# A hybrid encoder layer: where the first norm's scale is applied, and who orders TensorE in the first stage

## The chip, the cores and the metric

The kernel runs on one core of a Trainium2 chip. The metric is device time in microseconds (us) of one execution, with all inputs in device memory at the start. A core has TensorE (PE in the profile; its weight loads are PEld), VectorE (DVE), ScalarE (ACT), GpSimd (POOL) and SyncE (SP, which here only issues transfers). Each engine works through its own list of instructions in order; between engines, semaphores say when an operand is ready.

## The reference, cut to what matters

The layer is applied to 2048 prompt positions and, with the same weights, to 256 sample positions; the width is 1024.

```python
h = rmsnorm(x, norm1_w)                    # x * rsqrt(mean(x*x) + eps) * norm1_w
p = h @ w_in                               # mq, mk, mv, mo, gates, aq, ak, av
m_out = mlstm_mixer(mq, mk, mv, mo, gates, b_gates, mh_norm_w)   # 8 heads, both directions
a_out = attention_mixer(aq, ak, av, q_norm_w, k_norm_w)          # 8 heads, 2 kv heads, rotary
x = x + concat([m_out, a_out]) @ w_out
h = rmsnorm(x, norm2_w)
u = centred_dwconv(h @ w_up, conv_w, conv_b)
a, g = split(u, 2)
y = rmsnorm(x + (silu(g) * a) @ w_down, final_norm_w)
```

One head of the mLSTM, in one direction, at position l: with weights Dw and iw from the gates, and a state (C, n) carried over chunks,

```python
s = (q @ k.T) * Dw
num = iw * (q @ C) + s @ v
den = iw * (q @ n) + s.sum(-1)
h = num / max(abs(den), exp(-m))
out = sigmoid(mo) * rmsnorm_per_head(h_forward + h_backward) * mh_norm_w
```

The norm's scale r = rsqrt(mean(x*x) + eps) is one number for each position, and norm1_w one for each input column. So `(x*r*w1) @ W` is `r * (x @ (w1*W))`: r may be applied to x ahead of the products, or to the products' rows behind them.

## The kernel before, in words

All products are in float32 split into two parts: a high part (`fp32r`) and the remainder, and a product is the sum of three matmuls (high by high, high by low, low by high). The 2304 positions are 18 tiles of 128. The two sample tiles (16 and 17) come first, then the prompt tiles 0 to 15; x lies in memory transposed, so that a tile is [128 columns, 8 chunks, 128 positions].

**The first stage** (`phase_a`) works tile by tile. `front_a` loads x, squares it on ACT (L186), sums the eight chunks on POOL (`xq`, `sq`, L192, L193; for the first tile on DVE, L189), sums over partitions by a matmul with ones (`rs_a`, L131), takes the power -0.5 on POOL (`rcol_a`, L135) and spreads the result over all partitions by a second matmul with the identity (L142). `front_b` multiplies x by it on DVE (L200), makes the high part on ACT (L201) and the low part on DVE (L202), both called `n1T`, and stores them to memory for the mLSTM. `mm` projects a tile onto 800 columns (the attention's q, k, v and the gates, weights `w_a`) as 24 matmuls of 512 columns and 24 of 288 into `pj`, which has two buffers. `post_a` takes `pj` out of PSUM (`qk`, `v`, the gate columns `gtm`) and has the mean squares of the heads (`ms`, L267) turned into `rqk` on POOL (L100, L101). `post_b` scales by it (`xh`, L273), applies the rotary tables (`t`, L282 to L288) and splits the result (`qz`, L290, L291). `post2` turns the keys by PE (`pk`, L326); `gates` takes logarithms and turns the gates into rows (`pg`, L319). Into the same stage fall the split of the mLSTM's first weights (`wm`, L108 and L112) and the scaling of the rotary tables (`tab`, L232, mostly on POOL).

**The second stage** interleaves attention (`px`: score maxima, reduced by L570; `ps`: scores, L595 and L596; `pv`: values, L613) with the mLSTM in four passes of two heads. A pass projects all tiles again from the stored `n1T` (`proj`: `mj` holds k and q, `mv` holds v and the output gate), updates states (`upd`, `recur`), and produces outputs in steps `out_a` to `out_d`: products `mS`, `mI`, `mN` in one small PSUM pool (`pm`, tag "m", two buffers), a division and a norm on DVE, ACT and POOL (L886 to L919), and a turn `mT` with the gate applied (`mmx`, L931). The last pass (`p == LASTP`) projects transposed (`proj_kv`, `proj_qo`), so that its gate `ogT` has positions along the free axis. **Then** attention alone goes on beside the output projection (`po`), and the feed-forward stages (`pa` to `pd`) follow.

The order of the instructions on each engine is set when the program is built: a scheduler goes through the written program with modelled times and priorities and picks, on each engine, what is ready first. Where a scope says `manual_schedule` for PE, PE keeps the order of the source; before the change that scope begins only with the part in which attention runs alone.

## Time and profile before

| | |
|---|---|
| median of 3 runs | 3428.69 us (3424.76 to 3433.05) |
| the profiled execution's own time | 3428.88 us |
| its span, first to last instruction | 3427.2 us |
| PE busy | 3329.3 us (97%) |
| DVE busy | 2677.3 us (78%) |
| ACT busy | 1931.2 us (56%) |
| POOL busy | 1120.9 us (33%) |
| mean granted TensorE clock | 0.990 |

A busy time is the union of an engine's instructions; consecutive ones overlap a little, so the distance from start to start is the better measure of what one costs in a row of many. In lists of instructions, `[0.69 <-DVE mx L570]` says that the engine stood idle for 0.69 us before this one and that DVE's `mx` ended the wait. A row of a window table gives its length, then busy time and number of instructions of each engine, the granted clock, and the share and rate of the transfers.

### The profile page before, as it was taken

The page shows a single profiled execution, that of the slowest core. Times are in us where ns is not written, and L with a number is a line of the kernel's source. Part 1 is how long each engine was busy: PE and PEld are TensorE (multiplying, and loading weights), DVE is VectorE, ACT ScalarE, POOL GpSimd, SP SyncE. Part 2 cuts the span into 40 slices and gives each one's busy share as a digit, 9 for nine tenths or more (in the row PEclk, how much of TensorE's full clock was granted, in tenths as well). Part 3 has the DMA queues.
Part 4 walks back from the last instruction along what each step waited for, and adds up shares of the span by engine and source line. Part 5 has one row for each costly group of instructions (what it writes and reads, how often), then busy time and mean ns, then how long its engine had stood idle before and what let it go on. Part 6 is the DMA issues. An engine that isn't in the chain of part 4 may idle for free. (4 is left out here: it accounts for less than half of the span.)

```text
span 3427.2 us, 55596 instructions
## 1 busy us (share of the span) xinstructions
PE 3329.3 (97%) x20058; PEld 3098.4 (90%) x20058; DVE 2677.3 (78%) x4654; ACT 1931.2 (56%) x4329; POOL 1120.9 (33%) x1328
## 2 busy tenths in 40 slices
PE   7989999999999999899999999999999999999998
PEld 6878888888888888688899999999999999999998
DVE  6885687777768788967767878789888888888776
ACT  4536666666666767655544444446444446555554
POOL 6653132213232323211244333226233224322222
PEclk9999999999999999999999999999999999999999
DMA  6765342333345444422365232223323213421221
GB/s 220 243 203 159 89 140 86 115 123 98 108 131 160 143 123 139 145 77 94 101 216 198 81 105 87 68 80 133 129 94 103 72 59 128 140 74 62 69 74 50
DMA packets 254756, 404.27 MB, mean 118 GB/s; under 512 B 32112, under 2 KB 156816, under 8 KB 254480
## 3 DMA queue, kind: packets, MB, share of 16 engines
q1 hardware_dynamic: 226576, 358.23, 32.7%
q0 software_dynamic: 11344, 33.04, 3.6%
q10 hardware_dynamic: 16560, 9.44, 0.9%
q8 instruction: 158, 2.59, 0.3%
q14 instruction: 118, 0.97, 0.1%
HBM read 316.73 MB, written 83.90 MB: 117 GB/s over the span
## 5 line engine op out<-in xcount | busy, mean ns | idle before, releaser
L1322 PE MATMUL pd<-act,wd 128*128 128x384 f32 (+1 forms) x3120 | 593.4, 336 | 23.9 <-DVE acc L1324 12.6
L1322 PEld LDWEIGHTS pd<-act,wd 128*128 128x128 f32 x3120 | 539.6, 188 | 32.6 <-DVE acc L1324 18.1
L601 DVE TENSOR_TENSOR pl<-ps,ph 128x512 fp32r<-128x512 f32 x520 | 352.7, 683 | 181.5 <-ACT ps L600 173.4
L1184 PE MATMUL pa<-nt,wut 128*128 128x386 f32 (+2 forms) x2376 | 454.3, 339 | 0.0
L599 ACT ACTIVATE ph<-ps 128x512 fp32r<-128x512 f32 x520 | 309.4, 595 | 243.5 <-PE ps L596 239.5
L1184 PEld LDWEIGHTS pa<-nt,wut 128*128 128x128 f32 x2376 | 421.6, 190 | 0.3 <-ACT u L1200 0.3
L570 DVE TENSOR_REDUCE mx<-px 128x1 f32<-128x512 f32 (+1 forms) x528 | 345.5, 670 | 74.4 <-PE px L569 72.4
L1278 DVE SCALAR_TENSOR_TENSOR y<-u,cw,y 128x768 f32<-128x768 f32 (+1 forms) x264 | 315.6, 1196 | 36.4 <-ACT y L1271 29.3
L1189 POOL TENSOR_TENSOR tw<-ru 128x512 f32<-128x512 f32 x66 | 94.1, 1425 | 732.5 <-DMA ru<-w_up 558.5
L613 PE MATMUL pv<-ph,v 128*128 128x512 f32 (+1 forms) x1040 | 319.4, 401 | 1.0 <-ACT ph L599 0.8
L600 ACT ACTIVATE ps<-ps 128x512 f32<-128x512 f32 x520 | 310.3, 597 | 0.0
L1200 ACT ACTIVATE u<-pa 128x386 f32<-128x386 f32 (+2 forms) x264 | 128.3, 486 | 320.9 <-PE pa L1184 320.7
L1324 DVE TENSOR_TENSOR acc<-pd,acc 128x384 f32<-128x384 f32 (+1 forms) x544 | 280.3, 535 | 35.5 <-PE pd L1322 34.1
L1041 PEld LDWEIGHTS po<-cmx,wo 128*128 128x128 f32 x1728 | 220.7, 191 | 8.2 <-DVE mmx L931 0.6
L1041 PE MATMUL po<-cmx,wo 128*128 128x256 f32 x1728 | 224.2, 284 | 0.4 <-DVE mmx L931 0.4
L595 PE MATMUL ps<-qq,kk 128*128 128x512 f32 x520 | 215.5, 416 | 4.2 <-DVE mx L570 2.4
L569 PE MATMUL px<-kk,qq 128*128 128x512 f32 (+1 forms) x528 | 202.8, 413 | 6.0 <-DVE mx L570 2.9
L596 PE MATMUL ps<-qm,kl 65*128 65x512 f32 x520 | 206.7, 399 | 0.0
L759 PE MATMUL mj<-mn,wm 128*128 128x256 f32 x1296 | 203.0, 289 | 2.8 <-ACT og L773 1.9
L759 PEld LDWEIGHTS mj<-mn,wm 128*128 128x128 f32 x1296 | 187.1, 193 | 19.8 <-ACT og L773 2.0
L769 PEld LDWEIGHTS mv<-wm,mn 128*128 128x128 f32 x1296 | 182.8, 190 | 18.4 <-ACT qb L765 2.5
L769 PE MATMUL mv<-wm,mn 128*128 128x256 f32 x1296 | 196.5, 285 | 1.0 <-ACT qb L765 0.9
(288 smaller groups left out, 7266.6 us busy)
## 6 DMA issues: line engine op xcount, KB each, us to landing
ru<-w_up SPq DMA_DIRECT2D x132, 512.0 KB, 3.4
mn<-n_d SPq DMA_DIRECT2D x216, 256.0 KB, 3.4
rd<-w_down SPq DMA_DIRECT2D x66, 512.0 KB, 3.6
n_d<-n1T SPq DMA_DIRECT2D x18, 1024.0 KB, 5.6
dm<-nm_d POOLq DMA_DIRECT2D x72, 256.0 KB, 4.1
mjn<-n_d SPq DMA_DIRECT2D x72, 256.0 KB, 3.3
mvn<-n_d SPq DMA_DIRECT2D x72, 256.0 KB, 3.1
q_d<-qz SPq DMA_DIRECT2D x18, 512.0 KB, 3.7
```

Source lines behind the costliest of these rows:

```text
L570: nc.vector.tensor_reduce(s.mx[:, t, z0:z0 + 1], ps[:, 0:w], AX.X, ALU.max)
L599: nc.scalar.activation(ph, ps, AF.Exp)
L600: nc.scalar.activation(ps, ps, AF.Exp)
L601: nc.vector.tensor_tensor(pl, ps, f32(ph), ALU.subtract)
L613: nc.tensor.matmul(s.pv[0:HD if k in (1, 3) else P, 0:N], v, p, start=(kp == 0 and k == 0), stop=(2 * kp + 2 == s.nk and k == 5))
L759: nc.tensor.matmul(pj[:, o], s.w[c][:, a, o * P:(o + 1) * P], nT[c][:, :, h, :], start=(c + o + k == 0), stop=(c == NCC - 1 and k == 2 and ...
L769: nc.tensor.matmul(pv[:, o], nT[c][:, o, a, :], s.w[c][:, h, 256:512], start=(c + o + k == 0), stop=(c == NCC - 1 and k == 2 and o == 1))
L1041: nc.tensor.matmul(po[:, o], wo[z // 2][c][:, a, n], mx[c][:, h, :], start=(c == 0 and k == 0), stop=(c == NCC - 1 and k == 2))
L1184: nc.tensor.matmul(p, w[:, aa, c, :], ops[k][:, c, bb, 0:n], start=c == 0 and i == 0 and not add, stop=c == NCC // 2 - 1 and i == 2, skip_ ...
L1278: nc.vector.scalar_tensor_tensor(y[:, s:e], u[:, s + k:e + k], cw[:, k, jj:jj + 1], y[:, s:e], ALU.mult, ALU.add)
L1322: nc.tensor.matmul(po, wds[j][c // 4][:, aa, c % 4 * P:(c % 4 + 1) * P], acts[j][:, bb, z0:z1], start=(j == 0 and k == 0), stop=(j == len( ...
L1324: nc.vector.tensor_tensor(accs[c][:, z0:z1], po, accs[c][:, z0:z1], ALU.add)
```

## The change

Three things change together.

1. In the first stage `n1T` becomes the split of raw x. `front_a` and `front_b` become `load`, `squares`, `norm` and `parts`: `parts` needs nothing but the loaded x; `norm` sums the squares by the matmul with ones and leaves r as one column of a small tile `g.rt` [128 positions, 18 tiles]. The multiplication of x and the spreading matmul are gone. `post_a` applies r where it takes `pj` out of PSUM: as the scale of two ACT copies, and in two DVE instructions that become three-operand ones. The squares of the first tile too are summed on POOL.
2. The mLSTM's projections read the same stored raw x. v gets r squared (its own and k's), the column of ones beside v becomes r, and the bound exp(-m) is divided by r, which leaves q's factor out of the quotient. The output gate gets r/2 as the scale of its tanh: in the first three passes one 256-column ACT instruction becomes two of 128 columns, 27 times. In the last pass, where positions lie along the free axis, the gate is copied out of PSUM, r/2 is spread by two matmuls into a tile `mr` of the pool `pm`, DVE multiplies, and ACT takes the tanh in place, 9 times. The last pass's values are taken out by two ACT instructions in place of one, 9 times. `g.rh`, `g.r2` and `g.ri` are four small DVE instructions over 18 columns, once.
3. PE's order in the first stage is that of the source. The two sample tiles are projected together, chunk by chunk. From then on, in each tile's projection, the keys of the tile before last are turned between the 512-column and the 288-column half, with a pair of gate turns behind them, and the norm's matmul of the tile after next follows at the end. `gp` has four buffers. At the head the loads are issued in another order: the last two chunks of `w_a` come behind the rotary tables.

Over the whole program PE issues as many instructions as before: the 18 spreading matmuls of the first stage are gone, and the last pass has 18 for `mr`. DVE loses 18 multiplications of 128x1024 and one reduction and gains 9 multiplications of 128x256 and four small ones. ACT gains 45 instructions.

Three places show the order. On PE around the turn of the first keys, before (`pj2` is the projection of prompt tile 2, `pk16` the turn of sample tile 16's keys):

```order
L245 MATMUL pj2_715<-w_a6_134,n1T2_436 128x512 x3
L245 MATMUL pj2_715<-w_a7_135,n1T2_436 128x512 x3
L326 MATMUL pk16_415<-identr_75,qz16_339 128x128 x2
L131 MATMUL rs_a4_594<-ones_79,sq4_590 128x2
L245 MATMUL pj2_715<-w_a0_128,n1T2_436 128x288 x3
```

and after:

```order
L249 MATMUL pj0_455<-w_a6_139,n1T0_232 128x512 x3
L249 MATMUL pj0_455<-w_a7_140,n1T0_232 128x512 x3
L333 MATMUL pk16_480<-identr_75,qz16_382 128x128 x2
L249 MATMUL pj0_455<-w_a0_133,n1T0_232 128x288 x3
L249 MATMUL pj0_455<-w_a1_134,n1T0_232 128x288 x3
```

The turn of tile 16's keys has moved from within prompt tile 2 to within prompt tile 0, two tiles earlier. On DVE around one tile's head norm (`ms`), before:

```order
L267 TENSOR_REDUCE ms10_1_665<-qkq1_663 128x10
L258 TENSOR_TENSOR v2_772<-pj2_715,v2_772 128x128
L262 TENSOR_TENSOR gtm_98<-pj2_715,bgb_124 128x32
L288 TENSOR_TENSOR t1_0_559<-t1_0_559,t2_0_560 128x640
L200 TENSOR_TENSOR x4_586<-x4_586,rs_a4_594 128x1024
L291 TENSOR_TENSOR qz0_568<-t1_0_559,qz0_568 128x10x64
L200 TENSOR_TENSOR x5_701<-x5_701,rs_a5_709 128x1024
L202 TENSOR_TENSOR n1T4_670<-x4_586,n1T4_670 128x8x128
L273 TENSOR_TENSOR xh1_675<-qk1_655,rqk1_667 128x640
```

and after:

```order
L265 SCALAR_TENSOR_TENSOR v2_753<-pj2_684,rt0_88,v2_753 128x128
L269 SCALAR_TENSOR_TENSOR gtm_102<-pj2_684,rt0_88,bgb_128 128x32
L208 TENSOR_TENSOR n1T5_772<-x5_682,n1T5_772 128x8x128
L112 SCALAR_TENSOR_TENSOR wm0_4_795<-rm0_4_0_796,nw_81,wm0_4_795 128x512
L274 TENSOR_REDUCE ms10_2_761<-qkq2_759 128x10
L298 TENSOR_TENSOR qz1_669<-t1_1_660,qz1_669 128x10x64
L280 TENSOR_TENSOR xh2_776<-qk2_751,rqk2_763 128x640
```

Between a tile's `ms` and its `xh` DVE had seven instructions there, of which three are 128x1024; now it has one. On PE at the end of the mLSTM's last pass, before (`px`, `ps` and `pv` are attention's):

```order
L569 MATMUL px6_8_1_0_17475<-kk1_16_0_11354,qq6_8_17405 128x512
L926 MATMUL mT3_12_18335<-ident_70,hh3_12_18143 128x128
L901 MATMUL mN3_15_18340<-va3_7_13646,dm3_15_18119 128x65 x4
L569 MATMUL px6_8_2_0_17478<-kk1_16_0_11354,qq6_8_17405 128x512
L569 MATMUL px6_8_3_0_17481<-kk1_16_0_11354,qq6_8_17405 128x512
L883 MATMUL mS3_16_18359<-qb3_8_13648,mkT3_8_13647 128x256
L889 MATMUL mI3_16_18363<-C3_16_13621,qb3_8_13648 128x130 x2
L595 MATMUL ps4_8_1_0_17501<-qq4_8_17147,kk1_16_0_11354 128x512
L596 MATMUL ps4_8_1_0_17501<-qm4_8_17149,kl11_16_0_11355 128x512
```

and after:

```order
L967 MATMUL mT3_12_18377<-ident_70,hh3_12_18180 128x128
L942 MATMUL mN3_15_18382<-va3_7_13634,dm3_15_18156 128x65 x4
L924 MATMUL mS3_16_18401<-qb3_8_13636,mkT3_8_13635 128x256
L930 MATMUL mI3_16_18405<-C3_16_13609,qb3_8_13636 128x130 x2
L967 MATMUL mT3_13_18415<-ident_70,hh3_13_18303 128x128
L942 MATMUL mN3_16_18420<-va3_8_13637,dm3_16_18202 128x65 x4
L924 MATMUL mS3_17_18439<-qb3_8_13636,mkT3_8_13635 128x256
```

Between the last matmul of the pass's last projection (`mv3_8`) and `mT3_17`, its last turn, PE had 21 `px`, 28 `ps` and 30 `pv` of attention in its list; now it has none there, and they stand ahead of `mv3_8`. Up to `mT3_17` and from there on, both lists hold the same matmuls.

The diff, cut to its core:

```diff
-        def front_a(i):
+        def load(i):
             n = order.index(i)
...
-            xs[i] = x, rstd_bc(g, sf, pp if n else pj_, [sq], P, "rs" if n else "pj", f"a{i}", bufs=2)
+        def norm(i):
+            ps = pp.tile([P, 2], F32, tag="rs", name=f"rs{i}", bufs=2)
+            nc.tensor.matmul(ps, sqs.pop(i), g.ones, start=True, stop=True)
+            r = g.rt[:, i:i + 1]
+            nc.vector.tensor_scalar(r, ps[:, 0:1], EPS, None, ALU.add)
+            nc.gpsimd.tensor_tensor(r, r, g.mhalf[:, 0:1], ALU.pow)
+        def parts(i):
             nT = nTs[i] = sf.tile([P, NCC, 2, P], F32R, tag="nT", name=f"n1T{i}", bufs=3)
-            x, r = xs.pop(i)
-            nc.vector.tensor_tensor(x, x, r.unsqueeze(1).to_broadcast([P, NCC, P]), ALU.mult)
+            x = xs[i]
             nc.scalar.activation(nT[:, :, 0, :], x, AF.Copy)
...
-            nc.scalar.activation(qk, pj[:, 0:640].rearrange("p (h d) -> p h d", d=HD), AF.Copy)
+            nc.scalar.activation(qk, pj[:, 0:640].rearrange("p (h d) -> p h d", d=HD), AF.Copy, scale=rt)
...
-            nc.vector.tensor_tensor(v[:, 1], pv, f32(v[:, 0]), ALU.subtract)
+            nc.vector.scalar_tensor_tensor(v[:, 1], pv, rt, f32(v[:, 0]), ALU.mult, ALU.subtract)
...
+        st.enter_context(tc.manual_schedule(engines={mybir.EngineType.PE}))
         for n, i in enumerate(order):
-            pj, = mm(i)
-            if n:
-                post2(order[n - 1], prev)
+            if n == 0:
+                for k in range(2):
+                    bank(order[k])
+                mm(order[0:2], COLS)
+            elif n > 1:
+                bank(i)
+                mm((i,), COLS[0:1])
+            if n > 1:
+                post2(order[n - 2], kzs.pop(n - 2))
+                if steps:
+                    next(steps[0], None)
+                mm((i,), COLS[1:2])
+            if n + 2 < NT:
+                norm(order[n + 2])
...
+    def values(s, b, pv):
+        for o in range(2):
+            nc.scalar.activation(s.va[b][:, o, :, 0:64], pv[:, o, 0:P].rearrange("p (h d) -> p h d", h=2), AF.Copy,
+                                 scale=g.r2[:, 2 * b + o:2 * b + o + 1])
+        nc.gpsimd.tensor_copy(s.va[b][:, :, :, 64:65],
+                              g.rt[:, 2 * b:2 * b + 2].unsqueeze(2).unsqueeze(3).to_broadcast([P, 2, 2, 1]))
...
-        nc.scalar.activation(og, pj[:, 1], AF.Tanh, scale=0.5)
+        nc.scalar.activation(og, pj[:, 1], AF.Copy)
+        pr = pm.tile([P, 2, P], F32, tag="m", name=f"mr{s.p}_{b}")
+        for o in range(2):
+            nc.tensor.matmul(pr[:, o], g.rh[:, 2 * b + o:2 * b + o + 1].to_broadcast([P, P]), g.ident, start=True, stop=True)
+        nc.vector.tensor_tensor(og, og, pr.rearrange("p o t -> p (o t)"), ALU.mult)
+        nc.scalar.activation(og, og, AF.Tanh)
```

More of the change, by code (lines that the diff above doesn't have):

```diff
@@ L169, in phase_a @@
         bgb = cp.tile([P, 32], F32, name="bgb")
-        gps = [cp.tile([P, 2, 64], F32, name=f"gp{k}") for k in range(3)]
+        gps = [cp.tile([P, 2, 64], F32, name=f"gp{k}") for k in range(4)]
         ws = [wp.tile([P, 2, 800], F32R, name=f"w_a{c}") for c in range(NCC)]
@@ L350, in phase_a @@
                 after_mm()
-            qk, r = post_a(i, pj)
+            qk, r = post_a(i, pjs.pop(i))
+            if n + 3 < NT:
+                squares(order[n + 3])
             with ExitStack() as behind:
                 if n + 3 < NT:
-                    behind.enter_context(tc.issue_after(front_b(order[n + 3]).ins))
+                    behind.enter_context(tc.issue_after(parts(order[n + 3]).ins))
                     if n + 4 == NT:
@@ L357, in phase_a @@
                         after_x()
-                prev = post_b(i, qk, r)
-                if steps:
-                    for _ in range(2 if n == NT - 1 else 1):
-                        next(steps[0], None)
+                kzs[n] = post_b(i, qk, r)
                 if n < 7:
@@ L366, in phase_a @@
             if n + 4 < NT:
-                front_a(order[n + 4])
+                load(order[n + 4])
             if n == NT - 1:
@@ L1432, in body @@
             g.dec = ab.tile([P, 4, 2, NT], F32, name="dec")
+            g.rt, g.rh, g.r2, g.ri = (ab.tile([P, NT], F32, name=f"rt{k}") for k in range(4))
             sw = pool(s_wo, "m_w", bufs=1, side="right")
```

114 lines of the change are left out of this document (59 added, 55 removed).

## The prediction, made before the changed kernel ran

> **What bounds the kernel now.** I read the page's engine totals first, then a table of windows cut at the borders of the stages, then single waits. A window row gives its length, busy time and count of PE, PEld, DVE, ACT and POOL, granted clock, transfer share and rate.
>
> ```profile
> PE 3329.3 (97%) x20058; PEld 3098.4 (90%) x20058; DVE 2677.3 (78%) x4654; ACT 1931.2 (56%) x4329; POOL 1120.9 (33%) x1328
> ```
> ```profile
> 0.00:13.80 13.80, 1.36 (x4) 1.00 (x4) 7.41 (x9) 8.34 (x9) 4.84 (x14) 1.00 0.85 308
> 13.80:36.40 22.60, 21.92 (x104) 18.32 (x104) 15.46 (x27) 10.44 (x14) 21.20 (x37) 1.00 0.75 246
> 36.40:64.70 28.30, 23.07 (x109) 18.85 (x110) 17.25 (x30) 11.33 (x16) 14.21 (x16) 0.88 0.55 177
> 64.70:215.20 150.50, 140.83 (x771) 120.88 (x769) 131.30 (x269) 72.38 (x115) 100.52 (x78) 0.97 0.70 231
> 215.20:240.00 24.80, 18.41 (x135) 17.22 (x136) 19.72 (x47) 10.11 (x19) 15.22 (x39) 0.92 0.51 157
> 240.00:1380.00 1140.00, 1133.59 (x7238) 994.99 (x7238) 859.21 (x1867) 758.63 (x2031) 325.44 (x667) 1.00 0.43 126
> 1380.00:1400.00 20.00, 17.95 (x125) 15.89 (x123) 18.25 (x46) 13.50 (x39) 5.70 (x12) 1.00 0.74 220
> 1400.00:1420.00 20.00, 15.52 (x71) 12.02 (x70) 18.79 (x54) 12.00 (x36) 5.25 (x11) 0.75 0.24 66
> 1420.00:1440.00 20.00, 17.12 (x70) 11.55 (x68) 18.76 (x45) 12.13 (x33) 5.22 (x9) 0.91 0.07 20
> ```
>
> PE bounds the whole at 97%, and from 240 to 1380 it idles 6.4 us of 1140: there a us of PE work costs a us, and work on the others is covered. PE waits at two places that the change touches. One is the first stage: idle 12.4, 0.7, 5.2, 9.7 and 6.4 us in the first five rows, with DVE 87% busy between 64.7 and 215.2. The other is the end of the mLSTM, 1380 to 1440, where DVE is 93% busy and PE idles 2.0 + 4.5 + 2.9 = 9.4 us. From the last turn `mT3_17` on, PE's list is the same in both kernels, and I count that part as unchanged.
>
> **First stage, the pace.** The window from 64.7 to 215.2 holds the projections of prompt tiles 2 to 15, 14 tiles of 48 matmuls (the count of 673 in the first row here is one over): 150.5 / 14 = 10.75 us a tile. The second row is one tile at the stage's end, where the chain ahead of the projection has run out and PE never waits.
>
> ```profile
> 64.70:215.20 150.50, 135.75 (x673) 110.32 (x671) 0.97 0.70 231
> 206.07:215.16 9.09, 9.09 (x52) 7.82 (x50) 5.70 (x16) 3.21 (x6) 3.60 (x3) 1.00 0.95 346
> ```
> ```profile
> L200 DVE TENSOR_TENSOR x<-x,rs_a 128x1024 f32<-128x1024 f32 x12 | 14.5, 1208 | 0.2 <-PE rs_a L142 0.2
> L273 DVE TENSOR_TENSOR xh<-qk,rqk 128x640 f32<-128x640 f32 x15 | 15.8, 1052 | 8.9 <-POOL rqk L101 8.9
> L291 DVE TENSOR_TENSOR qz<-t,qz 128x640 fp32r<-128x640 f32 x15 | 13.3, 887 | 5.6 <-ACT qz L290 5.6
> L100 POOL TENSOR_SCALAR rqk<-ms 128x10 f32<-128x10 f32 x15 | 7.8, 519 | 31.3 <-DVE ms L267 31.1
> L142 PE MATMUL rs_a<-ident,rcol_a 128*128 128x128 f32 x24 | 5.3, 303 | 2.0 <-POOL rcol_a L135 1.9
> L131 PE MATMUL rs_a<-ones,sq 128*128 128x2 f32 x24 | 3.9, 232 | 6.5 <-POOL sq L193 3.4 <-DVE x L200 3.1
> ```
> ```profile
> 92.00 0.80 DVE L267 TENSOR_REDUCE ms<-qkq 128x10 f32<-128x640 f32 x1
> 92.89 0.24 POOL L100 TENSOR_SCALAR rqk<-ms 128x10 f32<-128x10 f32 x1 [0.51 <-DVE ms L267]
> 93.22 2.48 POOL L101 TENSOR_TENSOR rqk<-rqk,mhalf 128x10 f32<-128x10 f32 x1
> ```
>
> PE's floor for a tile is 9.1 us and the norm's matmul with ones, 3.9 / 12 = 0.3: 9.4 us. The spreading matmul and its waits are gone, as are the two waits of L131, since squares are now taken three tiles ahead. DVE works 131.3 / 14 = 9.4 us a tile; without L200's 1.2 us it is 8.2. But DVE's list now has only `qz` (0.9 us) between `ms` and `xh`, and `xh` needs `rqk`: 92.00 to 95.70 is 3.7 us, less `ms` (0.8) and `qz` leaves a wait of about 2.0, where it was 8.9 / 15 = 0.6. So DVE's pace is at most 8.2 + 2.0 = 10.2 us. It can be less: the copies of the gate turns fall into that wait, and the stretched rows (`xh` takes 0.81 us alone and 1.05 on average) have fewer neighbours. Between 9.4 and 10.2 I take 9.7, nearer to PE, because the split of `wm`, the heaviest addition, is in five of the 14 tiles only. 14 x (9.7 - 10.75) = **-14.7 us**; bounds -19 and, if nothing is won, 0.
>
> **First stage, the opening.** The pair of sample tiles needs the last two chunks of `w_a`, which were split by 20.4 us and now come behind two more megabytes (tables, the store of tile 16).
>
> ```profile
> 17.41 3.02 DVE L112 SCALAR_TENSOR_TENSOR w_a<-ra,nw,w_a 128x800 fp32r<-128x800 f32 x2
> 21.57 3.10 POOL L232 TENSOR_TENSOR tab<-tab,qkw 128x128 f32<-128x128 f32 x7
> 32.96 2.12 POOL L232 TENSOR_TENSOR tab<-tab,rot 128x128 f32<-128x128 f32 x5
> 70.11 0.29 PE L326 MATMUL pk<-identr,qz 128*128 128x128 f32 x2
> ```
>
> At the 308 GB/s of the first window two megabytes are 6 to 7 us, so both tiles end near 29, against 36.4 before for the second. Then PE comes to `pk16` in the middle of prompt tile 0, near 36, but its `qz` is late: POOL does the 28 table products first (21.6 to 35.1), then tile 16's `rqk` behind squares (near 41), then DVE's rotary work and ACT, 7 us more: near 48. PE, which may not pass `pk16`, stands some 12 us. The 7 us won are given back; adding the halves, prompt tile 1 ends near 64, as before (64.7). **-1 us**; bounds -8 (no stop) and +4 (tile 17's keys late in the same way).
>
> **First stage, the end.** Before, the projections' end was followed by the wait
>
> ```profile
> 218.16 0.34 PE L326 MATMUL pk<-identr,qz 128*128 128x128 f32 x2 [3.00 <-DVE qz L291]
> ```
>
> Now half of the mLSTM's first projection stands ahead of that turn. **-2 us** of the 6.4 idle; bounds 0 and -4.
>
> **The mLSTM.** 27 gates take two ACT instructions, and 9 values likewise:
>
> ```profile
> L773 ACT ACTIVATE og<-mv x27: 383/393/412, 237.7 to 1032.2; 128x256 f32<-128x256 f32 x27
> L772 ACT ACTIVATE va<-mv x54: 258/273/289, 235.9 to 1032.1; 128x128 f32<-128x128 f32 x54
> ```
>
> Each is 2 x 0.273 - 0.393 = 0.15 us longer, 5 us in all on an ACT that is 67% busy between 240 and 1380. They hold the only buffer of `mj`/`mv` longer; attention stands between on PE. **+0.5**; bounds 0 and +5. The column of ones becomes a POOL copy beside an idle POOL: 0. The 18 `mr` matmuls go into the stage that PE bounds. Their like is L142:
>
> ```profile
> 94.00 0.39 PE L142 MATMUL rs_a<-ident,rcol_a 128*128 128x128 f32 x2
> 94.14 6.61 PE L245 MATMUL pj<-w_a,n1T 128*128 128x288 f32 x36
> ```
>
> A pair of records is one matmul; with its loads it displaces some 0.25 us (the row group above gives 5.3 / 12 = 0.44 with overlaps). 18 x 0.25 = **+4.5**; bounds 0 and +8. DVE's 9 multiplications are covered until the end of the pass.
>
> **The end of the mLSTM.** Of the tail, DVE's rows between 1384 and 1440, its costliest first:
>
> ```profile
> L570 DVE TENSOR_REDUCE mx<-px 128x1 f32<-128x512 f32 x29 | 19.3, 677 | 0.0
> L601 DVE TENSOR_TENSOR pl<-ps,ph 128x512 fp32r<-128x512 f32 x14 | 9.4, 675 | 0.0
> L110 DVE TENSOR_TENSOR wo<-ro,wo 128x512 fp32r<-128x512 f32 x8 | 5.5, 683 | 0.3 <-ACT wo L108 0.3
> ...
> L630 DVE RECIPROCAL rs<-rs 64x128 f32<-64x128 f32 x4 | 3.5, 912 | 0.1
> ```
> ```profile
> 1404.05 1.94 PE L901 MATMUL mN<-va,dm 128*128 128x65 f32 x8 [3.11 <-DVE mmx L931]
> 1439.42 0.33 PE L926 MATMUL mT<-ident,hh 128*128 128x128 f32 x1
> 1405.53 0.22 POOL L100 TENSOR_SCALAR mr<-mms 128x2 f32<-128x2 f32 x1 [16.86 <-ACT s L913]
> 1405.83 0.99 POOL L101 TENSOR_TENSOR mr<-mr,mhalf 128x2 f32<-128x2 f32 x1
> ```
>
> The tail, from the start of `mv3_8` (near 1384.5) to `mT3_17`, took 55 us. Half of DVE's work there was attention's (19.3 + 9.4 + 3.5 for its reciprocals, of a sum of 63), and that has moved ahead of `mv3_8`, where DVE is 75% busy; PE's 79 attention matmuls have moved with it. What is left in the tail is about 26 us of DVE work (30 of the sum, at the 0.84 by which the sum overlaps), and nothing of attention to do while a tile's head norm goes through ACT and POOL (from `hh` to `mr` about 2 us, for each of the last four tiles, 7 us together) and the last turn. That is 34 us; with two PSUM buffers for all of it, one held by `mr3_8`, I take 36. PE's own work in it is some 20 us, so it idles 16, against 9.4: **+6.5 us**; bounds -3 (DVE's 26 us alone) and +25 (55 us, as long as before).
>
> Sum: -14.7 - 1 - 2 + 0.5 + 4.5 + 6.5 = -6.2. The profiled execution took 3428.88 us, 1.7 more than its span and 0.2 more than the median of 3428.69: **3422.7, say 3423 us**.
>
> The Trainium skill ("TensorE: Matmul & The Clock Gate", on what is actually happening) has a rule against this change: an idle window of some 3.4 us halves the PE clock until a window was busy. The trace agrees in kind: the granted clock is 0.75 in the 20 us that hold the 3.1 us wait. By that rule the stop at `pk16` and the bare tail would each be followed by 3.4 us at half speed, an estimate of 2 x 1.7 us, and the sum would be 3426 instead of 3423.
>
> **The rivals.** *The bare tail decides (slower).* `mr3_8` holds one of the two "m" buffers until DVE has multiplied `ogT8`, and that waits for `mmx` of tile 11; so `mT` 10, `mN` 13, `mS` 14, `mI` 14 and `mT` 11 pass one by one through the other, with no attention to fill PE. If the tail stays 55 us long, PE idles 35 and the term is +25: 3428.9 - 6.2 + 19 = 3442. It decides from a tail of 42 us on. Against it: DVE, 93% busy in the old tail, loses half its work. *DVE was the only brake (faster).* Relieved at both places, it lets the stage run at PE's 9.4 and the tail in its own 26 us: -1 - 19 - 2 + 0.5 + 4.5 - 3 = -20: 3409. For it speaks the 87% and 93%; against it the waits for POOL, which no row shrinks. *The change does not do what it says: the stage keeps its pace.* If squares on POOL (2.7 us a tile) get ahead of `rqk`, DVE waits 3 us a tile and the pace is near 10.6: -2 in place of -14.7, 3435.5. POOL waited 31 us for `ms` in these 14 tiles, so it mostly is free.
>
> **How the numbers follow.** The sum as worked out 0.38 (own range 3416 to 3430), bare tail 0.21, DVE the only brake 0.23, pace kept 0.18. A measurement here tells 0.2%, 6.9 us, from no change: 3421.8 and 3435.5. Faster: 0.23 and a little over half of 0.38, 0.20. Slower: 0.21, the greater part of 0.18, 0.11, and 0.01. That is 0.43, 0.24 and 0.33. The range 3407 to 3443 reaches to both outer rivals and leaves out half of each's spread at most.
>
> **What would show it.** Right: the first wide window's 14 tiles take 136 us, PE waits near 12 us once before its first key turn, `rqk` ends DVE's longest waits, and the tail from `mv3_8` to `mT3_17` has PE idle for about 16 us. Wrong: a pace under 9.4 or over 10.5 us, a first key turn without a wait, a tail outside 30 to 42 us, or a difference from 240 to 1380 beyond the 4.5 us of `mr`, which would be the scheduler's new order of attention and mLSTM and which I cost at nothing.

## The result: 34 us slower, and the profile after

The changed kernel takes 3460.26 us (median of 6 runs, 3456.0 to 3470.18), the kernel before on the same chip 3426.71: a ratio of 1.0099, with a 95% interval from 1.0083 to 1.0114. The forecast was 3423, with a range of 3407 to 3443. The profiled execution took 3458.37 us; its span is 3456.7, 29.5 us longer than that of before.

The engines' totals of the changed kernel, and a table of windows at the borders that the prediction used: the pair of sample tiles, prompt tiles 0 and 1, tiles 2 to 15, the stage's end, and the mLSTM up to the last pass's second projection (a row gives length, busy time and count of PE, PEld, DVE, ACT and POOL, granted clock, transfer share and rate):

```profile
PE 3338.7 (97%) x20058; PEld 3103.5 (90%) x20058; DVE 2671.2 (77%) x4648; ACT 1952.5 (56%) x4374; POOL 1112.0 (32%) x1332
```
```profile
0.00:30.80 30.80, 21.35 (x102) 18.11 (x102) 19.89 (x28) 16.71 (x19) 24.01 (x40) 1.00 0.94 325
30.80:66.70 35.90, 20.69 (x107) 17.67 (x107) 27.61 (x46) 17.12 (x25) 29.88 (x35) 0.81 0.61 196
66.70:218.00 151.30, 138.77 (x755) 118.28 (x753) 119.22 (x259) 71.00 (x108) 84.33 (x76) 0.97 0.69 220
218.00:240.00 22.00, 17.57 (x131) 17.05 (x132) 18.25 (x34) 9.95 (x18) 12.53 (x33) 0.92 0.47 151
240.00:1260.00 1020.00, 1012.00 (x6501) 890.94 (x6500) 749.91 (x1618) 690.59 (x1855) 295.67 (x606) 1.00 0.43 125
```

Tiles 2 to 15 took 151.3 us where they took 150.5. Nothing of the hoped-for 14.7 us is there. From 240 to 1260 PE still waits for almost nothing (8 us). The loss stands in the last pass. Here it is cut at the end of its projection `mv3_1`, the end of its last projection `mv3_8`, and its last turn `mT3_17`; first the kernel before, then the changed one:

```profile
1262.80:1393.60 130.80, 129.93 (x837) 114.32 (x836) 109.52 (x273) 91.35 (x243) 38.82 (x74) 1.00 0.51 150
1393.60:1439.70 46.10, 36.95 (x158) 26.39 (x157) 43.73 (x111) 27.20 (x76) 10.47 (x20) 0.85 0.20 57
1439.70:3427.20 1987.50, 1939.55 (x11443) 1887.71 (x11442) 1571.40 (x2269) 1022.63 (x2025) 623.30 (x449) 0.99 0.31 101
```
```profile
1256.20:1438.70 182.50, 173.56 (x980) 143.58 (x979) 148.84 (x341) 116.84 (x297) 43.41 (x82) 0.94 0.38 112
1438.70:1469.30 30.60, 20.09 (x77) 15.13 (x75) 19.43 (x66) 9.82 (x39) 5.53 (x12) 0.60 0.23 70
1469.30:3456.70 1987.40, 1938.47 (x11443) 1886.11 (x11442) 1571.00 (x2267) 1022.29 (x2022) 616.66 (x449) 0.99 0.31 101
```

The third row of each says that the part with the same list takes the same time, so the whole difference is made before `mT3_17`. The bare tail is indeed short, 30.6 us in place of 46.1. But the window of the seven projections ahead of it takes 182.5 us in place of 130.8. Not all of these 51.7 us are lost: 143 more matmuls fall into that window, most of them attention's that had filled the waits of the tail before.

Two things can make PE late: idle time, and a clock below full speed while it is busy (busy time, times one minus the granted clock, added up over windows of 10 us):

| place | PE idle, before and after | lost clock, before and after |
|---|---|---|
| to 240 us, the first stage | 34.4, 41.6 | 8.7, 8.3 |
| 240 us to the end of `mv3_1` | 5.6, 8.0 | 1.3, 0 |
| to `mT3_17`, the last pass | 10.0, 19.5 | 5.1, 18.2 |
| to the end | 47.9, 48.9 | 10.2, 9.3 |
| sum | 97.9, 118.0 | 25.3, 35.8 |

Idle time grew by 20.1 us and lost clock by 10.5, together 30.6 for a span that grew by 29.5. PE's own work did not grow: the 18 spreading matmuls of the first stage are gone, and the 18 of `mr` have come (each is two of the x36). The first row is of the kernel before, the second of the changed one:

```profile
L142 PE MATMUL rs_a<-ident,rcol_a 128*128 128x128 f32 x36 | 8.7, 324 | 5.4 <-POOL rcol_a L135 5.3
```
```profile
L849 PE MATMUL mr<-ident,rt 128*128 128x128 f32 x36 | 6.0, 276 | 0.2 <-DVE dm L927 0.2
```

What the last pass does now is seen in the changed kernel's PE timeline, at the ends of two of its projections (`mv3_5` and `mv3_8`):

```profile
1365.86 0.63 PE L822 MATMUL mv<-mvn,wm 128*128 128x256 f32 x4
1366.33 0.38 PE L849 MATMUL mr<-ident,rt 128*128 128x128 f32 x2
1366.55 0.27 PE L967 MATMUL mT<-ident,hh 128*128 128x128 f32 x1
1366.65 0.39 PE L849 MATMUL mr<-ident,rt 128*128 128x128 f32 x2
...
1369.68 1.10 PE L942 MATMUL mN<-va,dm 128*128 128x65 f32 x8 [1.14 <-DVE mmx L972]
...
1438.55 0.38 PE L849 MATMUL mr<-ident,rt 128*128 128x128 f32 x2
1438.77 0.27 PE L967 MATMUL mT<-ident,hh 128*128 128x128 f32 x1
1438.88 0.39 PE L849 MATMUL mr<-ident,rt 128*128 128x128 f32 x2
1440.93 1.11 PE L942 MATMUL mN<-va,dm 128*128 128x65 f32 x8 [1.67 <-DVE mmx L972]
```

A turn `mT` and the products `mN` of a tile come at once behind each projection, between and behind the two matmuls of `mr`. They are turns of tiles 4 and 10, which have nothing to do with the two projections' own tiles (10 and 11, 16 and 17). Before, `mT3_10` came at 1391.4, two us ahead of the end of `mv3_8`; now it comes at 1438.8, right behind it. What the buffer of `mr` then waits for stands in the rows of DVE and ACT behind the first of these places:

```profile
1380.45 0.27 DVE L972 TENSOR_TENSOR mmx<-mT,ogT 128x128 f32<-128x128 f32 x1
1380.75 0.38 ACT L846 ACTIVATE ogT<-mv 128x256 f32<-128x256 f32 x1 [5.77 <-DVE mmx L972]
1382.97 0.40 DVE L850 TENSOR_TENSOR ogT<-ogT,mr 128x256 f32<-128x256 f32 x1
```

`mr3_5` is written at 1366.33 and read, and so set free, only by the multiplication at 1382.97. The gate's copy `ogT` must come first; `ogT` has three buffers, and the one for this gate comes free with `mmx` of tile 5, whose turn stands behind this very `mr` in `pm`. So `mr` holds one of the two buffers while `mT` 4, `mN` 7, `mS` 8, `mI` 8 and `mT` 5 pass one by one through the other. The projections stand too: their single PSUM buffer is held until the same copy, and the first matmul of `mv3_6` starts at 1382.73. From the fourth of the nine `mr` on this takes 10 to 20 us each time, 91 us in all; the first three are read after 0.6 to 1.8 us. Outputs and projections take turns, where they ran side by side, and attention, which used to fill the outputs' waits, is done before the tail begins.

### The profile page after: what moved, and what is told of

It reads as the page before. It is cut to its first block, busy times and chain, and to the rows that moved or that the text cites. A ratio compares the mean times of both kernels' runs of the same rounds, so it can differ in the third digit from the quotient of the medians.

```text
span 3456.7 us, 55597 instructions
## 1 busy us (share of the span) xinstructions
PE 3338.7 (97%) x20058; PEld 3103.5 (90%) x20058; DVE 2671.2 (77%) x4648; ACT 1952.5 (56%) x4374; POOL 1112.0 (32%) x1332
## 5 line engine op out<-in xcount | busy, mean ns | idle before, releaser
L1365 DVE TENSOR_TENSOR acc<-pd,acc 128x384 f32<-128x384 f32 (+1 forms) x544 | 280.6, 536 | 37.2 <-PE pd L1363 35.8
```

Source lines behind the costliest of these rows:

```text
L1365: nc.vector.tensor_tensor(accs[c][:, z0:z1], po, accs[c][:, z0:z1], ALU.add)
```

## The experiments

Every ratio is to the kernel before in the same set of runs.

### What made the last pass slower

**The gate without r.** In the changed kernel's last pass:

```diff
-        nc.scalar.activation(og, pj[:, 1], AF.Copy)
-        pr = pm.tile([P, 2, P], F32, tag="m", name=f"mr{s.p}_{b}")
...
-        nc.vector.tensor_tensor(og, og, pr.rearrange("p o t -> p (o t)"), ALU.mult)
-        nc.scalar.activation(og, og, AF.Tanh)
+        nc.scalar.activation(og, pj[:, 1], AF.Tanh, scale=0.5)
```

> The last pass's gate without r: no spread tile mr, no multiplication by it, the tanh straight out of PSUM as before (the output gate of two heads then lacks r). Theory 'the buffer': mr takes its turn in the two-buffer pool pm, so the products of tiles that follow in the program wait until the gate's projection has come; that is what emptied the tail, and PE's list here has 84 attention matmuls behind mv3_8 again (79 before the change, none after it). It expects the 9.6 us of extra idle time and the 13 us of lost clock in the last pass to be gone: 3437 us (3432 to 3443). Rival 'the first stage': attention and mLSTM only shifted against each other because the first stage ends otherwise; then nothing changes here: 3455 to 3461.

Measured: 3428.37 us, 1.0006 (0.9996 to 1.0016). All of the loss is gone, more than the theory expected.

**r/2 from memory.** Here `g.rh` is stored once to memory, and each gate loads its 256 values spread over the partitions:

```diff
-        pr = pm.tile([P, 2, P], F32, tag="m", name=f"mr{s.p}_{b}")
-        for o in range(2):
-            nc.tensor.matmul(pr[:, o], g.rh[:, 2 * b + o:2 * b + o + 1].to_broadcast([P, P]), g.ident, start=True, stop=True)
-        nc.vector.tensor_tensor(og, og, pr.rearrange("p o t -> p (o t)"), ALU.mult)
+        rb = s1.tile([P, BT], F32, tag="og", name=f"rb{s.p}_{b}", bufs=1)
+        nc.sync.dma_start(rb, g.rh_d[2 * b:2 * b + 2].rearrange("n t -> (n t)").unsqueeze(0).to_broadcast([P, BT]))
+        nc.vector.tensor_tensor(og, og, rb, ALU.mult)
```

> The last pass's gate multiplied by r/2 that is loaded from memory, spread over the partitions by the transfer, instead of by mr on PE and in pm. All else as in the changed kernel. Theory 'the buffer': as without r, 3438 us (3433 to 3444), with 80 attention matmuls back in the tail. Rival 'the multiplication': DVE's product and the two ACT passes over the gate, which stay, are what delays the outputs: 3453 to 3461.

Measured: 3427.49 us, 1.0007 (0.9998 to 1.0016). This too is below the theory's range. The multiplication and the two ACT passes cost nothing that can be seen. In the last pass (from `mv3_1` to `mv3_8`, and to `mT3_17`) PE waits no longer than before, 0.8 and 8.8 us for 0.9 and 9.2:

```profile
1258.00:1394.60 136.60, 135.81 (x868) 118.85 (x867) 116.68 (x293) 95.79 (x256) 38.78 (x75) 1.00 0.52 153
1394.60:1441.00 46.40, 37.63 (x153) 26.54 (x152) 44.78 (x112) 27.08 (x75) 10.71 (x20) 0.82 0.19 58
```

The theory had left the extra idle time of the first stage in both sums. It is there: up to 240 us PE idles 44.5 us, 10.1 more than before, and over the whole span 11.6 more. But without the spreading matmuls and without `mr` PE's own work (busy time less lost clock) is 8.6 us less, and lost clock is 4.4 us less, so the two kernels stand level.

**The kernel before, with `mr` alone.** Its gate is copied out, multiplied by a spread column of ones, and the tanh taken in place:

```diff
-        nc.scalar.activation(og, pj[:, 1], AF.Tanh, scale=0.5)
+        nc.scalar.activation(og, pj[:, 1], AF.Copy, scale=0.5)
+        pr = pm.tile([P, 2, P], F32, tag="m", name=f"mr{s.p}_{b}")
+        for o in range(2):
+            nc.tensor.matmul(pr[:, o], g.ones[:, 0:1].to_broadcast([P, P]), g.ident, start=True, stop=True)
+        nc.vector.tensor_tensor(og, og, pr.rearrange("p o t -> p (o t)"), ALU.mult)
+        nc.scalar.activation(og, og, AF.Tanh)
```

> The kernel before, with nothing changed but the last pass's gate: copied out of PSUM, multiplied by a column of ones that two matmuls spread in a tile mr of pm, tanh in place (the result is the same). Theory 'the buffer': the tail's attention moves ahead here too (none of 79 left behind mv3_8), and the loss in the last pass comes alone: about +23 us and 4 for the 18 matmuls: 3453 us (3445 to 3460). Rival 'the first stage': +5 us for the matmuls, 3427 to 3435.

Measured: 3462.75 us, 1.0113 (1.0097 to 1.0128), a little above the range. This one edit has the whole loss, and its last pass looks like that of the changed kernel:

```profile
1264.20:1436.80 172.60, 163.65 (x955) 136.20 (x955) 142.29 (x329) 113.03 (x290) 43.50 (x82) 0.96 0.39 116
1436.80:1469.70 32.90, 21.26 (x78) 15.49 (x78) 19.82 (x67) 10.34 (x40) 5.41 (x12) 0.57 0.23 70
```

So the loss is `mr`, and neither the first stage nor its order. These three take away, or add, the matmuls, the tiles in `pm` and the binding to the projection together. Two more tell them apart.

**Spread ahead of the projection**, copied by DVE out of `pm` at once:

```diff
+        pr = pm.tile([P, 2, P], F32, tag="m", name=f"mr{s.p}_{b}")
+        for o in range(2):
+            nc.tensor.matmul(pr[:, o], g.rh[:, 2 * b + o:2 * b + o + 1].to_broadcast([P, P]), g.ident, start=True, stop=True)
+        rb = s1.tile([P, BT], F32, tag=("og", "kt")[b % 2], name=f"rb{s.p}_{b}", bufs=1)
+        nc.vector.tensor_copy(rb, pr.rearrange("p o t -> p (o t)"))
         pj = proj_halves(s, b, 256, "mv")
...
-        nc.vector.tensor_tensor(og, og, pr.rearrange("p o t -> p (o t)"), ALU.mult)
+        nc.vector.tensor_tensor(og, og, rb, ALU.mult)
```

> The changed kernel, with r/2 spread by the same two matmuls into the same pool pm, but written ahead of the gate's projection and copied by DVE to memory of the core (9 more DVE instructions of 128x256); the gate is multiplied by the copy. Theory 'the buffer is bound to the projection': mr's buffer is free again after one DVE copy, 75 attention matmuls are left in the tail, and the last pass loses nothing but the 18 matmuls and the copies: 3430 us (3426 to 3436). Rival 'more work in a full pool': 9 more tiles in two buffers and the matmuls are the loss, however they are placed: 3450 to 3463.

Measured: 3447.79 us, 1.0052 (1.0033 to 1.0070): between the two expectations. Here `mr` is read 0.6 to 4.5 us after it is written. By the ratios, unbinding gives back some 16 of the 34 us, and 18 are left, each known to within 6 to 8 us.

**The same, in the projections' own buffer** in place of `pm`:

```diff
-        pr = pm.tile([P, 2, P], F32, tag="m", name=f"mr{s.p}_{b}")
+        pr = pj_.tile([P, 2, BT], F32, tag="mj", name=f"mr{s.p}_{b}", bufs=MJ)
...
```

> As the one that spreads r/2 ahead of the gate's projection, but the spread uses the projections' PSUM buffer (mj) instead of one of pm's two; 72 attention matmuls are left in the tail. Theory 'turns in pm': the outputs of the last pass no longer share their two buffers with the spread: 3431 us (3427 to 3437). Rival 'the added work': the 18 matmuls and the copies cost what they cost there: 3442 to 3453.

Measured: 3440.05 us, 1.0040 (1.0025 to 1.0054). Again between. The windows from `mv3_1` to `mv3_8` and to `mT3_17`, first of the kernel that spreads ahead in `pm`, then of this one:

```profile
1264.10:1410.70 146.60, 143.76 (x899) 125.61 (x898) 125.12 (x305) 96.90 (x256) 38.87 (x74) 0.98 0.46 135
1410.70:1460.50 49.80, 38.29 (x157) 28.31 (x156) 43.75 (x111) 28.75 (x79) 10.75 (x20) 0.80 0.18 55
```
```profile
1267.00:1406.30 139.30, 137.51 (x872) 118.33 (x870) 117.38 (x288) 92.51 (x243) 38.20 (x72) 1.00 0.47 143
1406.30:1451.00 44.70, 33.96 (x144) 25.50 (x144) 39.37 (x101) 28.64 (x78) 10.37 (x20) 0.84 0.20 58
```

In steps of the ratios, from the kernel with r/2 from memory (1.0007): some 11 us for 18 matmuls and nine copies in the projections' buffer, of which 6 are the matmuls' own time; some 4 more for nine turns in `pm` (the two intervals overlap, so this step isn't sure); and some 16 more for a buffer that is held until its gate has been copied (1.0052 to 1.0099, intervals apart). With the spread unbound the tail is as long as before, 50 and 45 us, and with `mr` it is 31 and 33: the shift of attention comes with the binding. Why the 18 matmuls cost more than their own time is left open; the projections have a single buffer (`MJ` is 1), so the spread takes turns there too, and nothing here tells the matmuls from these turns.

### Where the first stage's gain went

All but the first start from the kernel with r/2 from memory. The places are of one profiled execution each.

**Keys behind the second half**, on the changed kernel:

```diff
-                post2(order[n - 2], kzs.pop(n - 2))
-                if steps:
-                    next(steps[0], None)
                 mm((i,), COLS[1:2])
+                post2(order[n - 2], kzs.pop(n - 2))
+                if steps:
+                    next(steps[0], None)
```

> In the first stage the keys of the tile before last and the gate turns stand behind the second half of a tile's projection, not between the halves. Theory 'the place of the turn': PE waited 10.7 us for qz there from tile 2 to 15, since qz stands behind the next tile's ms on DVE and has 6 us of PE's work to be ready; 3.5 us more make it ready in time, so the pace falls from 10.8 to about 9.8 us and the kernel to 3447 us (3443 to 3452). Rival 'DVE's own cycle': rqk on POOL, for which DVE waits 17.7 us in that stage, sets the pace, and PE only waits elsewhere: 3456 to 3461.

Measured: 3462.81 us, 1.0109 (1.0093 to 1.0124), no gain; the theory's range is missed, and the rival's is nearly met. What PE waits for in the stage (us in total, times, longest), in the changed kernel and then here:

```profile
PE pk L333 <- DVE qz L298: 10.7, 8, 2.0
```
```profile
PE pg L326 <- DVE rows L327: 7.9, 4, 3.5
PE pk L333 <- DVE qz L298: 2.9, 3, 1.7
```

The wait for `qz` is mostly gone, and the gate turns behind it wait in its place.

**The scheduler's own order on PE** (the `manual_schedule` line taken out).

> The kernel with r/2 from memory, with the first stage's PE order left to the scheduler instead of the source. Theory 'late qz': DVE makes qz behind the next tile's ms whoever orders PE, so PE's waits in the first stage change their place but not their sum (33 us of idle time to the end of tile 15's projection stay 28 to 38): 3424 to 3431. Rival 'the source's order': the order holds PE up at the first norms and keys; without it the stage ends 10 us earlier: 3417 (3413 to 3421).

Measured: 3425.81 us, 0.9997 (0.9988 to 1.0007), within the theory's range. Without the order of the source there is no stop behind the sample tiles, and prompt tile 1's projection ends at 51.4 us in place of 67.4; then the pace is slower, and the stage ends 7 us earlier, of which nothing clear of noise is left in the whole time:

```profile
30.20:51.40 21.20, 18.92 (x100) 15.94 (x100) 18.09 (x26) 13.28 (x20) 17.98 (x25) 1.00 0.60 198
51.40:212.40 161.00, 141.59 (x758) 122.29 (x758) 132.71 (x276) 74.92 (x115) 108.36 (x89) 0.94 0.77 219
```

**Forced orders on DVE and ACT**: `wm` also goes ahead of `post_b` in the program.

```diff
-                squares(order[n + 3])
+                with tc.issue_after(g.sq_ins):
+                    squares(order[n + 3])
...
-                    behind.enter_context(tc.issue_after(parts(order[n + 3]).ins))
+                    with tc.issue_after(g.sq_ins), tc.issue_after(g.ms_ins):
+                        lo = parts(order[n + 3]).ins
+                    behind.enter_context(tc.issue_after(lo))
```

> The kernel with r/2 from memory, with two orders forced in the first stage: on DVE the parts of the tile three on (n1T) and the split of wm come behind a tile's ms and ahead of its xh; on ACT the heads' squares come ahead of the square of x and of n1T. PE's order is that of the changed kernel. Theory 'late qz': ms no longer stands behind 3 us of DVE work and 2 us of ACT work, and POOL's rqk is covered by them, so qz is ready when PE comes to the keys; of the 12.5 us that PE idles from tile 2 to 15 most goes, pace 9.8 instead of 10.8 us: 3415 us (3411 to 3420). Rival 'latency': the chain from a projection's end to its keys is as long as before, 3424 to 3431.

Measured: 3427.83 us, 1.0002 (0.9992 to 1.0012), as the rival had it. PE waits less for `qz` (5.5 us for 12.6), and now the norm's matmul waits for POOL's sums:

```profile
PE rs L198 <- POOL sq L193: 7.8, 6, 3.5
PE pk L333 <- DVE qz L298: 5.5, 6, 1.8
```

**Both together**, the forced orders and the keys behind the second half.

> As the kernel with the forced orders on DVE and ACT, and the key turns behind the second half of a projection. Theory 'late qz': little left to win beside the forced orders, 3414 us (3410 to 3419). Rival 'latency': only 3.5 us more of slack help, so this is 8 us or more under the one with the keys between the halves.

Measured: 3435.13 us, 1.0025 (1.0016 to 1.0035), slower than either theory said.

**The opening**, on top of these:

```diff
-                post2(order[n - 2], kzs.pop(n - 2))
+                norm(i)
+                mm((i,), COLS[1:2])
+                if n > 2:
+                    if n == 3:
+                        post2(order[0], kzs.pop(0))
+                    post2(order[n - 2], kzs.pop(n - 2))
...
-                mm((i,), COLS[1:2])
-            if n + 2 < NT:
-                norm(order[n + 2])
```

> As the one before, and each tile's norm matmul stands between the halves of that tile's own projection, and tile 16's keys are turned together with tile 17's, one tile later. Theory: the stop of 13.8 us behind the pair of sample tiles is PE's order (it stands at the norm of prompt tile 1, whose squares POOL sums behind the tables); without it prompt tile 1's projection ends 8 to 12 us earlier and the kernel comes to 3405 us (3400 to 3411). Rival 'POOL and DVE': the chain to the first keys is the brake; PE only stops later, and nothing or up to 4 us is won against the one before.

Measured: 3439.23 us, 1.0040 (1.0025 to 1.0055), above both expectations. Prompt tile 1's projection ends at 50.1 us, 17 us earlier than in the kernel with r/2 from memory, and the stage ends 4 us earlier:

```profile
31.10:50.10 19.00, 18.21 (x103) 16.06 (x102) 16.45 (x32) 12.87 (x19) 17.63 (x24) 1.00 0.65 215
50.10:214.90 164.80, 139.40 (x758) 120.43 (x757) 130.23 (x271) 73.20 (x114) 101.87 (x89) 0.92 0.69 219
```

**Work left out**, to see what the stage hangs on.

```diff
-            return qk, rstd_of(g, sp, ms, 10, f"rqk{i}")
+            r = sp.tile([P, 10], F32, tag="rstd", name=f"rqk{i}")
+            nc.vector.tensor_scalar(r, ms, EPS, None, ALU.add)
+            return qk, r
```

> The kernel with r/2 from memory; in the first stage the power -0.5 of the heads' mean squares is left out, so that rqk is one small DVE instruction and DVE no longer waits for POOL between ms and xh (17.7 us from tile 2 to 15, and 3.5 us of latency in each tile's chain). Theory 'the loop over POOL': this wait is what fixes the stage's end near 218 us whatever the order of PE: end of tile 15's projection 8 to 14 us earlier, kernel 3416 (3411 to 3421). Rival 'DVE's amount': the waits turn into others, 3423 to 3429. Rival 'squares and loads': the same, 3423 to 3429.

Measured: 3423.55 us, 0.9992 (0.9983 to 1.0002): the stage ends 13 us earlier, as the first theory said, but the time is that of the rivals.

```diff
-                for q in range(2):
-                    sin = tab[:, ti, a, 1:2, :].rearrange("p h (r z f) -> p h r z f", r=2, z=2)[:, :, :, q, :]
-                    nc.vector.tensor_tensor(half(t2[:, h0:h1, :], q), half(xh[:, h0:h1, :], 1 - q),
-                                            sin.to_broadcast([P, n, 2, 16]), ALU.mult)
-            nc.vector.tensor_tensor(t1, t1, t2, ALU.add)
+            nc.vector.tensor_tensor(t1, t1, xh, ALU.add)
```

> The kernel with r/2 from memory; in the first stage the products with the sine half of the rotary tables are left out (t2; 1.36 us of DVE a tile, 24 us in all) and xh is added in its place. Theory 'DVE's amount': DVE's work and waits together are the pace, so 1.4 us a tile come off: 3415 us (3410 to 3420). Rival 'the loop over POOL': the chain of a tile is shorter by the same 1.4 us, but DVE waits longer for rqk: a gain under 5 us, 3422 to 3428. Rival 'squares and loads': 3424 to 3429.

Measured: 3429.56 us, 1.0015 (1.0005 to 1.0024), no gain, and just above all three ranges, though the stage ends 7 us earlier.

> Both of the above left out. If POOL's loop and DVE's amount brake one behind the other, this is under each of them alone; PE's own work, 9.7 us a tile, is then the pace: end of tile 15's projection 15 us earlier, 3410 us (3405 to 3416). If squares and loads are the brake, 3422 to 3429.

Measured: 3417.79 us, 0.9975 (0.9966 to 0.9985): the stage ends 20 us earlier, and the time is a little above the first range.

In the last, `squares` and `norm` are empty and `g.rt` is set to 1 once.

> The kernel with r/2 from memory; the norm's squares, their sums on POOL, the matmul with ones and the power are left out, r is 1 (3 us of POOL, 1.1 of ACT and 0.3 of PE a tile). Theory 'squares and loads': POOL's sums stand ahead of rqk and PE's stop behind the sample tiles is the norm of prompt tile 1: the 14 us stop shrinks by half or more, and the stage ends 10 us earlier: 3416 (3410 to 3421). Rival 'the loop over POOL' or 'DVE's amount': only 18 x 0.3 = 5 us of PE work go, 3420 to 3426.

Measured: 3425.85 us, 0.9999 (0.9990 to 1.0008), within the rival's range, with the stage's end 7 us earlier.

The windows of tiles 2 to 15 without the power, without the sine half, without both, and without squares, one row of each kernel:

```profile
68.00:206.60 138.60, 133.11 (x753) 113.99 (x753) 115.23 (x265) 70.60 (x109) 40.85 (x48) 1.00 0.81 234
```
```profile
69.40:212.00 142.60, 133.83 (x755) 113.84 (x753) 101.06 (x196) 70.05 (x108) 78.28 (x76) 1.00 0.79 227
```
```profile
63.20:199.60 136.40, 132.25 (x755) 114.43 (x754) 102.39 (x211) 70.74 (x109) 36.64 (x48) 1.00 0.82 243
```
```profile
70.30:212.00 141.70, 135.28 (x776) 116.90 (x774) 107.36 (x242) 61.54 (x99) 38.32 (x32) 1.00 0.72 230
```

All of the first stage in one table, with the pace over 14 tiles:

| kernel | tile 1 ends | tile 15 ends | us a tile | PE idle to 240 us |
|---|---|---|---|---|
| before | 64.7 | 215.2 | 10.75 | 34.4 |
| changed | 66.7 | 218.0 | 10.8 | 41.6 |
| r/2 from memory | 67.4 | 219.3 | 10.85 | 44.5 |
| keys behind the half | 65.7 | 218.8 | 10.9 | 42.0 |
| scheduler's PE order | 51.4 | 212.4 | 11.5 | 35.7 |
| forced DVE and ACT order | 64.3 | 219.2 | 11.1 | 41.0 |
| both | 63.0 | 218.1 | 11.1 | 43.5 |
| opening | 50.1 | 214.9 | 11.8 | 48.7 |
| no power | 68.0 | 206.6 | 9.9 | 35.2 |
| no sine half | 69.4 | 212.0 | 10.2 | 41.9 |
| neither | 63.2 | 199.6 | 9.7 | 29.8 |
| no squares | 70.3 | 212.0 | 10.1 | 42.1 |

Orders alone leave the stage's end between 212 and 219 us, though the openings differ by 17 us. What moves it as far or further is work taken out: the power 13 us, the sine half or the squares 7 each, the power and the sine half together 20. The chain from a projection through `ms`, `rqk`, `xh` and `qz` to the keys, with DVE and POOL in turn, fits this best, and PE's order decides mostly where PE waits for it. No run shows the chain alone: leaving out the power or the squares also takes POOL's busy time in these tiles from 84 us to some 40, and the pace is then nearly the same, 9.9 and 10.1. Without the sine half, which is DVE's, POOL is still busy for 78 us at 10.2, so POOL's amount of work is not all of it. Nor does the kernel keep what the stage wins: without the power it wins some 5 us of 13 by the ratios. From 240 to 300 us PE without the power is then busy for 52.7 us where it was 56.6 (the first row is of the kernel with r/2 from memory), and a wait for the mLSTM's loads has come up (from 205 to 285 us):

```profile
240.00:300.00 60.00, 56.58 (x440) 52.56 (x439) 33.31 (x64) 25.23 (x62) 35.34 (x84) 1.00 0.84 243
```
```profile
240.00:300.00 60.00, 52.68 (x354) 47.07 (x354) 29.78 (x59) 28.12 (x71) 32.78 (x76) 0.91 0.69 208
```
```profile
PE mj L791 <- DMA mn<-n_d: 5.1, 3, 2.5
```

No version that computes all of the layer was faster than the kernel before beyond the measurement. The kernel with r/2 from memory is level with it, in either PE order.

## Why the prediction was wrong, point by point

**The end of the mLSTM, +6.5: the step that failed.** The tail itself came out nearly as long as worked out, 39.5 us from the start of `mv3_8` for a forecast of 36, but partly by luck: PE idled 10.5 us in it for 16, and was busy 29.0 for some 20, mostly because the granted clock was 0.63 there. The step that failed lies ahead of the tail. The prediction took attention that "has moved ahead of `mv3_8`" as covered there, and the new order of attention and mLSTM from 240 to 1380 is one "which I cost at nothing". I looked for the price of `mr` behind the last projection only, and saw its buffer as a burden of `mr3_8`. But each of the nine `mr` is written behind its projection and ahead of the turns and products of later tiles, in a pool of two, and from the fourth on it holds its buffer for 10 to 20 us, until its gate is copied. So the outputs waited in the whole pass, in which PE idled 9.5 us longer and lost 13.1 us more of its clock. In the windows that is +51.7 us from `mv3_1` to `mv3_8`, less 15.5 in the tail and 6.6 that the mLSTM was ahead by then. The rival "the bare tail decides" had the right buffer, the right wait (`mmx` of tile 11) and the right sign, and 3442 for 3460, because it bound only the last pair; by its own condition, a tail of 42 us or more, it would not have decided.

**The clock.** By the prediction's sentence the clock gate would add 3.4 us. The last pass alone lost 13 us more than before. Rows of 5 us in the tail of the changed kernel:

```profile
1450.00:1455.00 5.00, 4.80 (x19) 3.69 (x18) 3.84 (x13) 1.28 (x6) 0.00 (x0) 0.50 0.02 5
1455.00:1460.00 5.00, 4.92 (x19) 4.08 (x19) 2.97 (x12) 0.59 (x4) 1.48 (x4) 0.50 0.08 23
1460.00:1465.00 5.00, 4.35 (x16) 3.20 (x15) 3.56 (x15) 0.59 (x4) 1.28 (x3) 0.50 0.07 18
```

PE counts as busy for 94% of these 15 us, in matmuls of 65 to 256 columns, and the clock stays at half. The Trainium skill ("TensorE: Matmul & The Clock Gate", on what is actually happening) has the clock back after about one busy window of 3.4 us; here the measurement differs. Its section on a second failure mode, with frequent short idles between groups of matmuls as they cycle through PSUM, is nearer to this row, though it speaks of a clock that swings. Which of the two is at work, no run here shows.

**First stage, the pace, -14.7.** Measured: +0.8 us over the 14 tiles. The step that failed is "DVE's pace is at most 8.2 + 2.0", with PE's floor as the only other limit. PE's floor is not 9.4 but 9.6: 138.8 us busy less 4.5 of lost clock, over 14, for the key and gate turns belong to it. And a pace worked out from one engine's work and one wait leaves out a loop, which the rows below show and no run here isolates. PE may not begin a second half before it has turned the keys of the tile before last; their `qz` stands on DVE behind the next tile's `ms`; and that `ms` waits for the projection that has only just ended (113.1 here). One turn of the loop in the changed kernel, on PE and then on DVE:

```profile
113.10 5.85 PE L249 MATMUL pj<-w_a,n1T 128*128 128x512 f32 x24
120.26 0.36 PE L333 MATMUL pk<-identr,qz 128*128 128x128 f32 x2 [1.31 <-DVE qz L298]
```
```profile
118.67 0.81 DVE L274 TENSOR_REDUCE ms<-qkq 128x10 f32<-128x640 f32 x1
119.40 0.81 DVE L298 TENSOR_TENSOR qz<-t,qz 128x640 fp32r<-128x640 f32 x1
```

The rival "the stage keeps its pace" was right in its outcome. Its reason, squares on POOL, is part of it at most: without them a tile takes 10.1 us, without the power 9.9.

**First stage, the opening, -1.** Measured +2.0 at the end of prompt tile 1 (66.7 for 64.7), within the bounds; the sample tiles end at 30.8, where 29 was forecast. PE does stop once, for 13.8 us where 12 were forecast, but at another place:

```profile
44.72 0.59 PE L198 MATMUL rs<-ones,sq 128*128 128x2 f32 x2 [13.84 <-POOL sq L193]
45.16 7.42 PE L249 MATMUL pj<-w_a,n1T 128*128 128x512 f32 x24
52.41 0.29 PE L333 MATMUL pk<-identr,qz 128*128 128x128 f32 x2
```

It is the norm's matmul of prompt tile 1, two tiles before it is needed, whose squares POOL adds behind the tables; by then the first keys are in time. I had overlooked that this matmul stands ahead of prompt tile 0's projection. The sum was right by luck, though the first key turn came without a wait, one of the prediction's signs of being wrong. The same POOL list makes both late, and in the opening experiment, with that stop gone, the time was lost further on.

**The small terms.** The stage's end: idle 6.4 to 4.4 us, -2.0 for -2. ACT's splits: from 240 us to `mv3_1` idle rose by 2.4 us and lost clock fell by 1.3, and with the splits kept and `mr` gone the kernel is level, so +0.5 stands within what can be told. The `mr` matmuls: 6.0 us by their row, for 4.5; the 8.7 that went with the spreading matmuls more than balance them.

## What to carry to other kernels

A small tile in a PSUM pool of two is not priced by its matmuls: ask what must be done before its buffer comes free, and which tiles stand behind it in the program's order. Here `mr` waited for work that itself stood behind `mr` in the pool, and all of it went through one buffer in place of two; a value that can come from memory or be made ahead keeps the two apart. And a stage whose waits move whenever an order is changed, while its end stays, probably hangs on a chain through several engines: price the chain, not the wait.

## What was not expected of the hardware

In the changed kernel's tail the granted clock stood at 0.50 for at least 15 us on end while PE counted as busy for 94% of them, in small matmuls with short waits between. Lost clock made up a third of the loss, 10.5 of 30.6 us. And 18 matmuls whose row says 6.0 us cost some 11 with their copies even outside `pm`.
